# The memory projection moved behind the queries of tile zero, and all background work laid out in tables of slots

## The chip, the cores and the metric

The kernel runs on one core of one Trainium2 chip. The metric is the time of one execution on the device in microseconds (us). The core has five engines that run side by side: TensorE (PE, matmuls), VectorE (DVE), ScalarE (ACT), GpSimd (POOL) and SyncE (SP, which issues most of the DMA transfers, in order). The profile's granted clock is the share of TensorE's full speed that it was allowed.

## The reference

A decoder layer with one input projection, three groups of heads, a gate and an output projection, for 2048 rows of width 1024 in float32:

```
h = rms_norm(x, pre_norm_g);  proj = h @ w_in
a_u, a_v, sq, sk, sv, mq, z = split(proj)          # 512, 512, 256, 128, 128, 256, 1024 columns
y_a = gelu(a_u) * spatial_gating(gelu(a_v))        # A: layer norm per 128 channels, then causal 128x128 mixing over rows
y_b = sliding_window_attention(sq, sk, sv)         # B: 4 heads of 64, window 128, sinks, relative bias
mk, mv = split(rms_norm(mem, mem_norm_g) @ w_mem_kv)
y_c = memory_cross_attention(mq, mk, mv)           # C: 4 heads of 64 over 256 memory rows
y = concat(y_a, y_b, y_c) * silu(z)
out = x + rms_norm(y @ w_out, post_norm_g)
```

## The kernel before

The 2048 rows are worked in four tiles of 512 (L20). Every float32 operand of a large product is split into a high and a low part (ACT casts the high part, L107; DVE subtracts it, L108), and each product is three matmuls per 128 of depth: high by high, high by low, low by high. A unit is one such product of 128 output columns by a tile of 512 rows, 24 matmuls with a 128x512 result. The memory's units (gm, L494) have 256 columns of rows only.

Each tile runs its units in a fixed order: four units of v (L1076, with the rows as the stationary operand), sv, k, q0, q1, mq0, mq1 and the gates z4 to z7 (all in `group`, L388). In tile 0 the four memory units (`project_memory`, L487) stand between z5 and z6. Behind z7 of tiles 1 and 3 comes `set_a`: the u and z columns of group A, for two tiles together, with a Strassen-like scheme (28 products X, Y, Z at L819) on sums of blocks of h and of weights. The output projection (L1383) ends the kernel, with the same scheme, as a phase of its own from about 622 us.

The order on PE and SP is the order of the program. ACT, DVE and POOL are ordered by the language's scheduler, which lists each engine's instructions ahead of time from its own estimates, within the order that the data sets.

Background work hangs on slots. `slot()` is called after every 6 matmuls of a unit (about 1.4 us of PE). It sends the stores that have come due (`store_later` gives each a number of ticks), runs the jobs that are registered for this slot (`add_jobs`), and then the attention steps for it. Slot 0 of a tile is the start of its q1, and slots -28 to -1 are the tile's v, sv, k and q0. The jobs are: the row statistics of the next tile (`next_stats`: load a piece of x as xs, square and sum it on ACT at L311, reciprocal root on POOL, two small transfers), the raw rows of the next tile (`load_x`, xk and xj) and their scaling and splitting into h (`make_h`, L371), sums of h blocks (`h_sums`, hd and hr) and of weights (`weight_sums`, tu and tz), first sums of y (`first_sums`, ya at L767, ys2), operands of the output weights (`weight_operands`, wo, L697), and the operands of the last phase (`y_operand`). An attention unit has three steps: logits and softmax, transposes into pT, and the product with the values into OB or OC. B runs 4 units and C 8 per tile, and C of a tile runs on under v, sv and k of the next tile.

Weights come through a ring. `weight_unit` (L224) is called as a unit starts. It frees the place of the unit before, takes the raw weights of a later unit into that place, and issues the next raw load; there are three ring places and, in tile 0, a fourth (s4a), and three raw tiles. In tile 0 a raw block of 0.5 MB is loaded (L197), split, and its split form of 1 MB is stored to split_d (L243); tiles 1 to 3 load the split form at once (L205), which a place can only take when its former unit is done. All these transfers stand in SP's one queue with the jobs' transfers, in the order of the program; where SP waits for one transfer's data or place, all behind it wait.

In names, `hs` are the four resident buffers of split rows, `s4a` and `s4b` two spare ones. `wraw_0_8` is the raw weight of unit 8 in tile 0; units 0 to 3 are v, 4 sv, 5 k, 6 and 7 q, 8 and 9 mq, 14 to 17 z4 to z7, and 30 to 33 the memory's. `xs_1_4` is piece 4 of the rows of tile 1 for their statistics.

## Time and profile before

| | |
|---|---|
| runs shown | 787.1, 786.89, 782.41 us; median 786.89 |
| profiled execution | 783.41 us, span 781.7 us |
| mean granted clock | 0.984 |
| busy over the span | PE 746.3 us, DVE 576.8, ACT 481.4, POOL 93.4 |
| data moved by DMA | 220.19 MB, mean 282 GB/s |

The profile is one execution. Busy times are sums per engine; PE is busy for 95% of the span, so its idle time, and the time in which its clock was granted less, are the two quantities to follow. A row of the timeline shows when an instruction (or a run of like ones) began, how long it took, its engine, line and tiles, and in brackets how long the engine had been idle and what ended that. A row of waits shows who waited for what, with the total in us, the number of times and the longest.

### The profile page before, as it was taken

Reading aid. Unit: us, or ns where it says so; the run is one execution under the profiler, and the core shown is the slowest. Engines: PE = TensorE matmul, PEld = TensorE weight load, DVE = VectorE, ACT = ScalarE, POOL = GpSimd, SP = SyncE. Lnnn points to the kernel's source line nnn. Section 1 sums busy time; section 2 is a strip of 40 time slices with the busy share of each in tenths; the row PEclk is TensorE's granted clock in tenths of the full one; section 3 lists DMA queues with packets and bytes.
Section 4 is the critical chain, followed back from the end, with each engine's and each line's share of the span. In section 5 each row is a group of like instructions: output and inputs, shape, how many; then the busy total and the mean of one; then the engine's idle time right before and its main releaser. Section 6 shows DMA issues by size and latency. Waiting matters only on the chain.

```text
span 781.7 us, 10655 instructions
## 1 busy us (share of the span) xinstructions
PE 746.3 (95%) x3604; PEld 620.7 (79%) x3604; DVE 576.8 (74%) x1070; ACT 481.4 (62%) x1048; POOL 93.4 (12%) x115
## 2 busy tenths in 40 slices
PE   9999989889899999989998989999999999999996
PEld 7878968668778888867886768888887888888884
DVE  6665887588986779833797876898658818677587
ACT  7796856984479954236575795588853334434441
POOL 0110212110221000010043010141000000010011
PEclk9999989999999999999999999999999999999999
DMA  8999298996894587789979969986457889547824
GB/s 326 354 337 395 92 408 316 368 325 216 312 318 139 181 280 263 264 296 388 371 280 359 354 243 337 366 295 215 152 184 251 281 335 405 212 145 282 329 106 188
DMA packets 80646, 220.19 MB, mean 282 GB/s; under 512 B 7723, under 2 KB 16464, under 8 KB 72144
## 3 DMA queue, kind: packets, MB, share of 16 engines
q1 hardware_dynamic: 75456, 210.54, 74.6%
q10 hardware_dynamic: 5136, 8.98, 3.1%
q8 instruction: 28, 0.46, 0.2%
q14 instruction: 26, 0.21, 0.1%
HBM read 153.42 MB, written 66.07 MB: 281 GB/s over the span
## 4 chain that ended last, share of the span: by engine, by line
PE 53%; DMA 16%; DVE 14%; ACT 12%; issue 2%; SPq 2%; POOL 1%; DVEq 0%; ACTq 0%; POOLq 0%
PE X L1383 11%; PE X L819 11%; PE Y_S L1383 6%; PE Y L819 5%; DMA ring<-split_d 4%; PE Y L1383 3%; PE Z L819 3%; PE g_q L388 2%; PE v L1076 2%; PE g_mq L388 2%; DMA xp<-in_x 2%; DMA wraw_a<-in_wst 2%; PE sg L785 1%; DVE hs L108 1%; ACT G_v L1103 1%
## 5 line engine op out<-in xcount | busy, mean ns | idle before, releaser
L1076 PE MATMUL v<-ring,hs 128*128 128x512 f32 x336 | 86.6, 409 | 7.9 <-DMA ring<-split_d 3.6
L388 PE MATMUL g_z<-hs,ring 128*128 128x512 f32 x360 | 88.0, 394 | 3.6 <-DMA ring<-split_d 3.6
L1076 PEld LDWEIGHTS v<-ring,hs 128*128 128x128 f32 x336 | 64.3, 197 | 23.6 <-DMA ring<-split_d 4.0
L388 PEld LDWEIGHTS g_z<-hs,ring 128*128 128x128 f32 x360 | 65.9, 188 | 17.0 <-DMA ring<-split_d 4.2
L819 PE MATMUL X<-hs,ring 128*128 128x512 f32 x288 | 71.4, 395 | 0.0
L819 PEld LDWEIGHTS X<-hs,ring 128*128 128x128 f32 x288 | 52.3, 188 | 10.2 <-DVE hs L108 0.2
L388 PE MATMUL g_mq<-hs,ring 128*128 128x512 f32 x192 | 45.0, 390 | 0.0
L388 PE MATMUL g_q<-hs,ring 128*128 128x512 f32 x168 | 42.7, 405 | 1.5 <-DMA ring<-split_d 1.5
L108 DVE TENSOR_TENSOR ring<-wraw_a,ring 128x1024 fp32r<-128x1024 f32 x28 | 35.4, 1263 | 11.1 <-ACT ring L107 9.8
L388 PEld LDWEIGHTS g_mq<-hs,ring 128*128 128x128 f32 x192 | 35.8, 188 | 7.3
L594 POOL TENSOR_SCALAR_AFFINE_SELECT pT_b<-pT_b 128x512 fp32r<-128x512 f32 x30 | 25.9, 862 | 126.1 <-ACT pT_b L107 126.0
L1276 POOL TENSOR_TENSOR r<-a,mhalf 128x1 f32<-128x1 f32 x16 | 12.8, 802 | 231.5 <-DVE a L1274 226.8
L388 PEld LDWEIGHTS g_q<-hs,ring 128*128 128x128 f32 x168 | 31.6, 193 | 8.2 <-DMA ring<-split_d 1.9
L108 DVE TENSOR_TENSOR ring<-wraw,ring 128x1024 fp32r<-128x1024 f32 (+1 forms) x18 | 21.6, 1202 | 16.8 <-ACT ring L107 16.7
L1383 PE MATMUL Y_S<-hs,yop 128*128 128x512 f32 x144 | 33.1, 389 | 0.0
L107 ACT CAST ring<-wraw_a 128x1024 fp32r<-128x1024 f32 x28 | 29.3, 1047 | 5.0 <-DMA wraw_a<-in_wst 3.9
L581 ACT ACTIVATE Lc_b<-Lc_b,nm_b 128x129 f32<-128x129 f32 x64 | 25.0, 395 | 11.8 <-DVE nm_b L579 11.5
L1383 PEld LDWEIGHTS Y_S<-hs,yop 128*128 128x128 f32 x144 | 27.0, 188 | 5.6
L1383 PE MATMUL X<-hs,yop 128*128 128x512 f32 x120 | 30.4, 389 | 0.0
L1383 PE MATMUL X<-hs,ring 128*128 128x512 f32 x120 | 30.4, 389 | 0.0
L1244 ACT ACTIVATE junk<-oa 128x512 f32<-128x512 f32 x16 | 10.1, 633 | 32.8 <-DVE oa L1430 23.6
L1240 DVE TENSOR_TENSOR yop<-y,yop 128x1024 fp32r<-128x1024 f32 x10 | 12.2, 1221 | 24.0 <-ACT yop L1235 24.0
(277 smaller groups left out, 1823.5 us busy)
## 6 DMA issues: line engine op xcount, KB each, us to landing
ring<-split_d SPq DMA_DIRECT2D x38, 1024.0 KB, 8.0
split_d<-ring SPq DMA_DIRECT2D x11, 1024.0 KB, 10.0
wraw<-in_wst SPq DMA_DIRECT2D x21, 512.0 KB, 5.8
hs<-wo_B SPq DMA_DIRECT2D x8, 1024.0 KB, 9.8
y<-yd SPq DMA_DIRECT2D x8, 1024.0 KB, 6.0
xs<-in_x SPq DMA_DIRECT2D x24, 256.0 KB, 7.8
hd_S<-h SPq DMA_DIRECT2D x24, 256.0 KB, 4.6
hrS<-hd_S SPq DMA_DIRECT2D x24, 256.0 KB, 4.8
```

The costliest lines, as they stand in the source:

```text
L107: a = nc.scalar.copy(hi, src)
L108: b = (lo_engine or nc.vector).tensor_tensor(lo, src, f32(hi), ALU.subtract)
L388: nc.tensor.matmul(ps, w[:, wi, k * P : (k + 1) * P], h(t, hi, k), start=(n == 0), stop=(n == 3 * KC - 1))
L581: nc.scalar.activation(Lc[:, h, : P + 1], Lc[:, h, : P + 1], AF.Exp, bias=nm[:, h : h + 1], accum_out=den[:, h : h + 1])
L594: nc.gpsimd.affine_select(prev[:, s], f32(own[:, s]), [[0, 4], [-1, P]], ALU.is_gt, 0.0, base=0, channel_multiplier=1)
L785: nc.tensor.matmul(pg[:, i, :], vg[:, i, :], wsp[:, g, :], start=True, stop=True)
L819: nc.tensor.matmul(banks[g], w[:, wi, k * P : k * P + P], at_slot(places[op], hi, k), start=first and i == 0, stop=i == 11, skip_group_che ...
L1076: nc.tensor.matmul(vps[i], h(t, hi, 2 * j + kk)[:, i * P : (i + 1) * P], w[:, wi, kk * 512 : (kk + 1) * 512], start=(j == 0 and (hi, wi, k ...
L1240: nc.vector.tensor_tensor(w[:, 1], yraw[name, p][:, 2 * half : 2 * half + 2], f32(w[:, 0]), ALU.subtract)
L1244: nc.scalar.activation(junk, o[:, c], AF.Square, accum_out=ss[:, col : col + 1])
L1276: nc.gpsimd.tensor_tensor(r, a, mhalf2[:, 0:1], ALU.pow)
L1383: nc.tensor.matmul(banks[m], a(s, k)[:, m * P : (m + 1) * P], w(v, k), start=first and n == 0, stop=n == 11, skip_group_check=not first)
```

## The change

Three things are changed; each matmul, each transfer and each step of ACT and DVE stays what it is, but for ACT's loads of function tables, which follow from its order.

First, the memory projection (`memory_along`, `project_memory`) in tile 0 stands right behind q1, in slots 4 to 11, so that mq0, mq1 and z4 to z7 follow it. The order of the weights is changed with it. The splitting of the memory rows into mT (`next(prep)`), which stood ahead of mq0 and mq1, stands behind sv and behind k.

Second, all slots of background work are numbers in tables, where formulas set them before. `STATS`, `SQUARES` and `RSTD` replace a common list with an offset for each tile; `A_STARTS`, `A_TURN` and `A_END` give each attention unit its three steps; `H_SUMS`, `H_LOADS`, `H_OPS`, `H_SPARE`, `T_SLOTS`, `T_STEPS`, `Y_SUMS`, `Y_OPS`, `Y_WEIGHTS` and `WO_LOADS` those of the sums and operands. `LOADS`, `MAKES`, `MIX_SLOTS` and `WO_SLOTS` exist before and have other numbers.

Third, `STORE_AFTER` goes from 6 to 11, and `PUT_OFF` and `H_STORE` give each kind of store its own ticks.

```diff
-STORE_AFTER = 6
+STORE_AFTER = 11
-TURN_SLOT = 30
+TURN_SLOT = 19
...
-NEXT_STATS = (-8, 18, -23)
+STATS = ((-10, -6, 0, 1, 5, 8, 12, 15), (18, 21, 25, 28, 33, 35, 39, 42), (-23, -24, -16, -12, -9, -5, 0, 1))
...
-MAKES = ((32, 33, 35, 36, 38, 39, 41, 42), (66, 68, 70, 72, 76, 79, 85, 88), (20, 22, 24, 26, 29, 31, 33, 35))
+MAKES = ((33, 34, 36, 37, 39, 40, 42, 39),
+         (65, 67, 68, 71, 75, 78, 84, 87),
+         (17, 19, 21, 23, 26, 28, 30, 32))
...
         order += [(U_V + j, t) for j in range(4)] + [(U_SV, t), (U_K, t), (U_Q, t), (U_Q + 1, t)]
-        order += [(U_MQ, t), (U_MQ + 1, t), (U_Z + 4, t), (U_Z + 5, t)]
         if t == 0:
             order += [(U_MK, t), (U_MK + 1, t), (U_MV, t), (U_MV + 1, t)]
-        order += [(U_Z + 6, t), (U_Z + 7, t)]
+        order += [(U_MQ, t), (U_MQ + 1, t)] + [(U_Z + 4 + i, t) for i in range(4)]
...
         for n in range(12):
-            aw, dw, bw, cw, am, bm, cm = A_SLOTS[t]
-            a, b, c = (aw + dw * n, bw, cw) if n < 4 else (am + 3 * (n - 4), bm, cm)
+            a, b, c = A_STARTS[t][n], A_TURN[t][n], A_END[t][n]
...
         SB.append(split_heads(slotted(U_Q + 1, f"q{t}_1", False), f"q{t}_1", "S1"))
         slot()
+        if t == 0:
+            memory_along()
+            project_memory(late["mT"], slot)
         for i in range(2):
-            if t == 0:
-                late["mT"] = next(prep)
             SC.append(split_heads(slotted(U_MQ + i, f"mq{t}_{i}", False), f"mq{t}_{i}", f"S{2 + i}"))
...
-        gate_bc(0)
-        gate_bc(1)
-        if t == 0:
-            memory_along()
-            project_memory(late["mT"], slot)
-        gate_bc(2)
-        gate_bc(3)
+        for i in range(4):
+            gate_bc(i)
```

What the tables do is read from the order of the instructions. The first place is ACT during the v units of tile 1. `G_v1_0` to `G_v1_3` are the gelus of v's four row blocks, `L_c` the softmax of attention C of tile 0, and an `ACT_TABLE_LOAD` loads the function table that the next step needs. Before:

```order
L660 ACT_TABLE_LOAD
L660 ACTIVATE G_v1_0_1510<-v_1_0_1231 128x512
L632 ACT_TABLE_LOAD
L632 ACTIVATE L_c0_1_1_1443,den_c0_1_1_1445<-l_c0_1_1_1438,nm_c0_1_1_1444,rsr_x0_273 128x256 x2
L660 ACT_TABLE_LOAD
L660 ACTIVATE G_v1_1_1533<-v_1_1_1232 128x512
L107 CAST pT_c0_0_0_1429<-tp_c0_0_1_1467 128x2x256
L549 ACTIVATE L_c0_1_1_1443<-L_c0_1_1_1443,den_c0_1_1_1445 128x256 x2
L1103 ACTIVATE G_v1_0_1510<-G_v1_0_1510,nb_1_0_1526,rsr_v1_0_1524 128x128 x4
L632 ACT_TABLE_LOAD
L632 ACTIVATE L_c0_2_0_1490,den_c0_2_0_1492<-l_c0_2_0_1485,nm_c0_2_0_1491,rsr_x0_273 128x256 x2
```

And now:

```order
L696 ACT_TABLE_LOAD
L696 ACTIVATE G_v1_0_1518<-v_1_0_1228 128x512
L696 ACTIVATE G_v1_1_1541<-v_1_1_1229 128x512
L145 CAST pT_c0_0_0_1461<-tp_c0_0_0_1456 128x2x256
L585 ACTIVATE L_c0_1_1_1432<-L_c0_1_1_1432,den_c0_1_1_1434 128x256 x2
L145 CAST pT_c0_0_0_1461<-tp_c0_0_1_1464 128x2x256
L696 ACTIVATE G_v1_2_1564<-v_1_2_1230 128x512
L696 ACTIVATE G_v1_3_1587<-v_1_3_1231 128x512
L668 ACT_TABLE_LOAD
L668 ACTIVATE L_c0_2_0_1488,den_c0_2_0_1490<-l_c0_2_0_1483,nm_c0_2_0_1489,rsr_x0_273 128x256 x2
L689 COPY oh_c0_0_1_1514<-o_c0_0_1_1509 64x512
```

All four gelus stand between two table loads; before, four loads are in the rows shown, and two more surround the gelus of `G_v1_2` and `G_v1_3` further down.

The second place is SP's queue at the start of tile 2's sv. `ring0` from `split_d` (first of the two) is the weight of sv, `ya` are parts of y read back for the first sums. Before:

```order
L306 DMA xs_3_0_3321<-in_x 128x512
L767 DMA ya_11_3329<-yd_107 128x2x512
L767 DMA ya_21_3330<-yd_107 128x2x512
L767 DMA ya_22_3331<-yd_107 128x2x512
L205 DMA ring0_84<-split_d_88 128x2048
L306 DMA xs_3_1_3348<-in_x 128x512
L205 DMA ring1_85<-split_d_88 128x2048
```

And now:

```order
L343 DMA xs_3_1_3315<-in_x 128x512
L343 DMA xs_3_0_3323<-in_x 128x512
L242 DMA ring0_84<-split_d_88 128x2048
L802 DMA ya_11_3357<-yd_107 128x2x512
L802 DMA ya_21_3358<-yd_107 128x2x512
L802 DMA ya_22_3359<-yd_107 128x2x512
L242 DMA ring1_85<-split_d_88 128x2048
```

The weight's load has moved ahead of the three `ya` loads, and `xs_3_1` ahead of it.

The third place is SP's queue in tile 0, under q and the units that follow it. Before:

```order
L243 DMA split_d_88<-ring2_86 128x2048
L306 DMA xs_1_2_576<-in_x 128x512
L197 DMA wraw_0_15_593<-in_wst 128x1024
L243 DMA split_d_88<-s4a_87 128x2048
L306 DMA xs_1_3_616<-in_x 128x512
L197 DMA wraw_0_30_639<-in_wst 128x1024
L243 DMA split_d_88<-ring0_84 128x2048
L306 DMA xs_1_4_662<-in_x 128x512
L197 DMA wraw_0_31_685<-in_wst 128x1024
L243 DMA split_d_88<-ring1_85 128x2048
```

And now:

```order
L280 DMA split_d_88<-ring2_86 128x2048
L234 DMA wraw_0_33_607<-in_wst 128x1024
L280 DMA split_d_88<-s4a_87 128x2048
L343 DMA xs_1_2_617<-in_x 128x512
L343 DMA xs_1_3_626<-in_x 128x512
L234 DMA wraw_0_8_652<-in_wst 128x1024
L343 DMA xs_1_4_680<-in_x 128x512
L234 DMA wraw_0_9_692<-in_wst 128x1024
L234 DMA wraw_0_14_730<-in_wst 128x1024
L343 DMA xs_1_5_745<-in_x 128x512
```

The memory's weights (30 to 33) have come ahead of those of mq (8, 9) and of the gates (14 and on), with no store of a split block behind them, and the reloads of `xs` stand at other places among them.

More of the change, by code (lines that the diff above doesn't have):

```diff
@@ L323, in from_dram @@
             nc.sync.dma_start(late["bcs", t], rstd_d[t : t + 1].broadcast_to([P, TS]))
-        for n, s in enumerate((0, 3, 7, 10, 14, 17, 21, 24)):
-            yield s, lambda n=n: load(n)
-            yield s + 6, lambda n=n: square(n)
-        yield 31, rstd
-        yield 33, to_dram
-        yield 36, from_dram
+        for n in range(8):
+            yield STATS[t - 1][n], lambda n=n: load(n)
+            yield SQUARES[t - 1][n], lambda n=n: square(n)
+        for s, job in zip(RSTD[t - 1], (rstd, to_dram, from_dram)):
+            yield s, job
     def along(rstd, t):
@@ L703, in operand @@
                     split(w[:, 0, c], w[:, 1, c], r[raw][:, c])
-            store_later(wo_d[op][j], f32(w), 4)
+            store_later(wo_d[op][j], f32(w), PUT_OFF[0])
         def difference(new, a, b, at):
@@ L911, in combine @@
             if name:
-                store_later(hsum_d[p][name][k], r[into, k], 2)
+                store_later(hsum_d[p][name][k], r[into, k], H_STORE[p])
         def operand(name, slot, k):
@@ L1127 @@
         slot()
+        if t == 0:
+            late["mT"] = next(prep)
         ps = group(weight_unit(U_K, t), t, f"k{t}", ps_t)
@@ L1136 @@
         slot()
+        if t == 0:
+            late["mT"] = next(prep)
         def values():
```

122 lines of the change are left out of this document (72 added, 50 removed), and 19 rows, old and new, of tables (A_END, A_STARTS, A_TURN, H_SUMS).

## The prediction

> **What bounds the kernel now.** I read the page's busy shares first, then the busy time by stage, then the list of what TensorE (PE) waited for, and last the timeline at each wait.
>
> ```profile
> PE 746.3 (95%) x3604; PEld 620.7 (79%) x3604; DVE 576.8 (74%) x1070; ACT 481.4 (62%) x1048; POOL 93.4 (12%) x115
> core 0: us, PE busy (x) PEld busy (x) DVE busy (x) ACT busy (x) POOL busy (x), PEclk, DMA share, GB/s
> 0.00:100.00 100.00, 98.47 (x500) 83.34 (x501) 67.38 (x150) 78.50 (x157) 12.57 (x23) 1.00 0.82 302
> 100.00:180.00 80.00, 70.16 (x328) 55.72 (x328) 61.77 (x142) 60.61 (x130) 12.73 (x13) 0.94 0.91 339
> 180.00:340.00 160.00, 156.42 (x787) 131.74 (x786) 123.79 (x201) 94.34 (x217) 14.99 (x19) 1.00 0.74 250
> 340.00:420.00 80.00, 72.42 (x335) 59.79 (x334) 54.11 (x128) 48.12 (x122) 17.41 (x20) 0.96 0.94 347
> 420.00:600.00 180.00, 174.64 (x878) 145.71 (x877) 141.27 (x270) 129.66 (x296) 22.91 (x24) 0.99 0.78 275
> 622.00:782.00 160.00, 152.22 (x672) 125.72 (x670) 108.51 (x153) 62.53 (x117) 12.83 (x16) 0.99 0.67 252
> ```
>
> PE is the bound: it is idle 781.7 - 746.3 = 35.4 us. Of that 7.8 lies in the last stage, the output projection, which the change doesn't touch, and 1.5 ahead of the first matmul. About 26 us are left, spread over four stages (9.8, 3.6, 7.6, 5.4). After some of the waits the granted clock is below 1, so that the matmuls behind them are slow as well. The changed kernel issues the same matmuls, so these waits and their slow matmuls are all that it can win, and new waits are all that it can lose.
>
> ```profile
> PE g_z L388 <- DMA ring<-split_d: 3.6, 2, 2.4
> PE v L1076 <- DMA ring<-split_d: 3.6, 1, 3.6
> PE v L1076 <- ACT hs L107: 2.6, 2, 1.7
> PE svt L1141 <- DVE OC L655: 2.6, 1, 2.6
> PE g_sv L388 <- DMA ring<-split_d: 2.5, 1, 2.5
> PE l_c L622 <- ACT L_c L632: 2.5, 2, 1.9
> PE v L1076 <- DVE hs L108: 1.6, 3, 0.8
> PE Y L819 <- DVE s4b L108: 1.6, 1, 1.6
> PE g_q L388 <- DMA ring<-split_d: 1.5, 1, 1.5
> PE g_k L388 <- ACT L_c L632: 1.4, 1, 1.4
> PE o_c L650 <- ACT pT_c L107: 1.2, 1, 1.2
> ```
>
> These are total, count and longest. There are two kinds: weights that land late (ring<-split_d), where SyncE's (SP's) single queue issued them late, and background steps on ACT and DVE (h, exp, OC) that end late. Both hang on the order in which slots issue work, which is what the change lays out anew.
>
> ```profile
> 111.74 4.11 PE L1076 MATMUL v<-ring,hs 128*128 128x512 f32 x9 [0.41 <-DVE hs L108]
> 346.41 7.41 PE L388 MATMUL g_sv<-hs,ring 128*128 128x512 f32 x24 [2.52 <-DMA ring<-split_d]
> 353.66 5.60 PE L388 MATMUL g_k<-hs,ring 128*128 128x512 f32 x24
> 415.88 2.86 PE L1076 MATMUL v<-ring,hs 128*128 128x512 f32 x6 [3.57 <-DMA ring<-split_d]
> ```
>
> The same 24 matmuls take 5.60 us undisturbed and 7.41 behind a wait of 2.52: the slow clock costs 1.8 on top. By the same rate nine should take 2.1 and took 4.11 (2.0 lost), six should take 1.4 and took 2.86 (1.5 lost).
>
> For this there is a rule. The Trainium skill, "TensorE: Matmul & The Clock Gate", in "Why this matters for your kernels", says that the clock drops where TensorE idles for over about 3 us. By that rule waits of 0.4 to 2.5 us would cost no clock, and removing them would not bring the slow matmuls back. The trace differs: 7.41 against 5.60 behind 2.52 us. The rows decide, and the rule's outcome is a rival below.
>
> **The change part by part.** The places go in order of time; each ends with a value and its bounds.
>
> (1) Tile 1's first product, 106 to 116. The waits for h are 3.5 (2.6 + 1.6, less 0.8 of tile 3), and the clock 2.0.
>
> ```profile
> 106.25 1.03 ACT L107 CAST ring<-wraw 128x1024 fp32r<-128x1024 f32 x1
> L108 DVE TENSOR_TENSOR hs<-xk,hs 128x512 fp32r<-128x512 f32 x16 | 12.0, 756 | 0.4 <-ACT hs L107 0.3
> ```
>
> A 1.03 us weight cast stands right ahead of the first h cast on ACT; in the new order it stands two copies and a softmax step earlier, and the memory values' steps (L523/L524), which lie among them before, are long done. On DVE the two low halves of h (0.76 each) still stand behind z7's scaling, which needs the end of z7, so about 1.3 us of wait stays. Gain 3.5, bounds 1.5 and 5.5.
>
> (2) Attention C of tile 0, under v, sv and k of tile 1, 140 to 172. That is 9.8 - 3.5 = 6.3 us of idle (l_c and svt the largest).
>
> ```profile
> 140.00:150.00 10.00, 7.75 (x37) 5.71 (x36) 4.71 (x18) 9.35 (x21) 2.02 (x2) 1.00 1.05 399
> 150.00:160.00 10.00, 9.09 (x45) 6.83 (x43) 8.05 (x32) 8.57 (x17) 1.58 (x2) 1.00 0.96 358
> 160.00:170.00 10.00, 6.81 (x28) 5.22 (x28) 9.72 (x22) 9.91 (x26) 0.82 (x1) 0.84 0.84 278
> L660 ACT ACT_TABLE_LOAD x8 | 10.3, 1283 | 0.1
> L632 ACT ACT_TABLE_LOAD x5 | 6.4, 1283 | 0.1
> ```
>
> ACT is busy 27.8 of 30 us here. Six of its steps are table loads of 1283 ns, since gelu and exp alternate; in the new order the four gelus of tile 1 stand together and two loads are left, so ACT has 4 x 1.28 = 5.1 us less to do ahead of the steps that PE waits for. The clock of 0.84 over 6.81 busy us costs 1.1. DVE is full from 160 on and still carries h sums, so I don't take all of 7.4: gain 5, bounds 2.5 and 7.4.
>
> The Trainium skill, "ScalarE: Activation LUTs", in "What ACT_TABLE_LOAD costs", adds a drain of about 1.38 us to each load of 1.28. By that, as an estimate, four loads would be worth 10.6 us of ACT, all of this place's 7.4 would go, and the sum below would be 2.4 lower. The trace agrees on the load (1283), and shows 0.2 us of idle before all thirteen loads of these two lines, so no drain.
>
> (3) z5 and z7 of tile 1, 199 to 218: 3.6 us for late weights.
>
> ```profile
> 193.73 0.32 SPq L205 DMA_DIRECT2D ring<-split_d  x1
> ring<-split_d SPq DMA_DIRECT2D x38, 1024.0 KB, 8.0
> ```
>
> z5's load left SP at 193.73 and landed 8.0 later, at 201.7, just as PE started. Ahead of it stood four h loads and the loads tu_3 and tz_3; now two of the h loads and those two stand behind it, but h sums of k=2 still stand ahead of z7's load. Gain 2.5, bounds 0 and 3.6.
>
> (4) sv and q1 of tile 2, 343 to 367: 2.5 + 1.5 of wait, 1.8 of clock.
>
> ```profile
> 336.47 1.99 SPq L767 DMA_DIRECT2D ya<-yd  x3
> 338.55 0.41 SPq L205 DMA_DIRECT2D ring<-split_d  x1
> ```
>
> sv's load stood behind three ya loads, which SP held until 336.47 for their data, and left at 338.55, 5.3 us before PE needed it. In the new order it stands ahead of them. What it needs then is only its place, which the second product of v gave up two units of about 5.5 before 343.9, at 333; so the wait of 2.5 and its clock go. q1's load now stands behind xs_3_3 and xs_3_4, so its 1.5 may stay. Gain 4, bounds 1.5 and 5.8.
>
> (5) v of tile 3 at 412: 3.6 of wait, 1.5 of clock.
>
> ```profile
> SPq L360 <- DVE hs L108: 25.9, 5, 9.4
> 407.87 1.07 SPq L205 DMA_DIRECT2D ring<-split_d  x1
> ```
>
> The load left at 407.87, behind xk_3_2, which waited for DVE to make h of k=0. That step is three slots earlier now and ahead of two weight subtractions: about 4 us. Gain 4, bounds 2 and 5.1.
>
> (6) Attention C under tile 3's v, sv and k: 0.8 + 1.2 + 1.4. The makes of h are earlier, and the last two gelus stand behind an exp and the svs copy, which releases pT_c and L_c sooner. Gain 3, bounds 0 and 3.4.
>
> (7) Y at 593: 1.6 for s4b. Its DVE step now follows the addition into u directly, without the two steps that stood between. Gain 1.5, bounds 0 and 1.6.
>
> (8) The memory projection, now right behind q1 in tile 0.
>
> ```profile
> L494 PE MATMUL gm<-hs,ring 128*128 128x256 f32 x72 | 9.3, 285 | 0.0
> split_d<-s4a SPq DMA_DIRECT2D x3, 1024.0 KB, 10.1
> 54.28 11.04 PE L388 MATMUL g_mq<-hs,ring 128*128 128x512 f32 x48
> SPq L306 <- ACT xs L311: 43.7, 12, 7.9
> ```
>
> Its matmuls are half as wide: a unit lasts about 3 us, where one of mq lasts 11.04 / 2 = 5.5. Four units therefore use up four weight blocks in 12 us, not 22, and the fourth (gm_3) gets the place of q1's weights, whose store takes 10.1 us to land. That store comes into SP's queue as q1 starts, one unit ahead of 54.28, at about 48.5, behind one raw load; landed by 59 to 60, it lets ACT cast at 60 to 61. gm_3 starts three units of 3 behind 54.28, at 63.3, and a cast and a subtraction (about a microsecond each, as at place 1) lie between: 0 to 1.5 us late. I take 1.5, the late end, since a late load slows the clock too. Nothing below zero is possible, since this stage has no wait at present (98.5 busy of 100, with 1.5 before the first matmul). The work on mT stands where it stood on ACT and DVE, hidden under sv and k; I cost it at nothing, as I do the stores that leave 11 ticks behind their step rather than 6: they only hold their tiles longer, and PE doesn't read those. Without that cover it is one of the waits of (9).
>
> (9) New waits that I haven't named: nearly every background step moves, so one load will come late somewhere; the rows above give 2.4 to 3.6 for one. Take one, 3, bounds 0 and 6 (two).
>
> Sum against the profiled execution's own 783.4 (span 781.7 and 1.7 around it): 3.5 + 5 + 2.5 + 4 + 4 + 3 + 1.5 = 23.5 of gain, 1.5 + 3 = 4.5 of loss: 783.4 - 19.0 = 764.4. The profiled execution lies 3.5 below the median of the runs shown (786.89) and 1.0 above their lowest. I add half of the 3.5: **766**. One per cent, about what a measurement of this kernel can tell from no change, puts the bounds at 779.0 and 794.8.
>
> **The rivals.** *Nearly all goes.* Every gain at its upper bound, 32.4, and no new wait: 783.4 - 32.4 = 751.0, and with the same 1.7 about 753. For it speaks that most waits are below 3 us; against it that DVE is busy 9.72 of 10 at 160. Chance 0.07.
>
> *The waits go, the slow clock stays.* The clock terms are 2.0 + 1.1 + 1.8 + 1.5 = 6.4; at the share taken above, about 5 of them would not come back: 771. It decides if slow stretches come without waits ahead of them. Against it stands that every slow stretch found follows a wait. This is the outcome by the clock rule of the Trainium skill named above. Chance 0.07.
>
> *Other waits in their place.* DVE, not ACT, sets the end at (1), (2), (5) and (6): 9.72 of 10 busy there. Then their 15.5 shrinks to 4, (3), (4) and (7) give 8, and a denser start and later stores bring 9 of new waits: 783.4 - 12 + 9 = 780. It decides where DVE's steps in that order end no earlier than before. Chance 0.16.
>
> *SP blocks the weights.* SP issues in order, and a reload of xs waits for ACT's square of the tile's previous content: 43.7 us over 12 times, up to 7.9. In the new order xs_1_4 stands ahead of the raw loads of mq1 and z4, behind the square of xs_1_2, which stands behind gm_3's late cast on ACT. If that hold reaches 7.9, with about 2 us to spare, mq1 starts 5.9 late, plus 1.8 of clock: 7.7. The same pair (xs ahead of a weight load) is set in tiles 1 and 2: three times make 23, and with only (3) and (4) gained (6.5) that gives 783.4 + 23 - 6.5 = 800. It decides from 2 us of hold, and pays above 795 once the three holds together pass 18. For it speaks the 43.7; against it that those waits cost PE nothing in tile 0 at present. Chance 0.10.
>
> **How the numbers follow.** The forecast itself has 0.60, with a range of its own of 756 to 777 (gains and losses don't reach their ends together). Faster by over 1%: 0.60 + 0.07 + 0.07 = 0.74; within 1%: 0.16; slower: 0.10. The range 755 to 784 leaves out the case where nearly all goes and the slower one, 0.17, and reaches through most of the case in which other waits take over.
>
> **What would show it.** In the changed kernel's profile: twelve table loads' rows in place of sixteen, two of them at 140 to 160; sv of tile 2 and v of tile 3 with no wait for ring<-split_d over 1 us, and 24 matmuls of sv in about 5.6; z5 of tile 1 likewise; under 2 us of wait ahead of tile 1's first h; and in 54 to 75 at most 1.5 of idle. PE idle in all about 17, not 35. I would be wrong if PE waits for gm or mq weights in 60 to 80 for more than 3 us, if svt still waits for OC at 165, or if the idle time adds up to 30 with other names in it.

## The result, and the profile after

The changed kernel takes 761.3 us (median of 4 runs, 760.16 to 765.02) beside 784.65 for the kernel before (782.0 to 787.1): a ratio of 0.9711, with a 95% interval of 0.9657 to 0.9766. The profiled execution took 760.56 us with a span of 758.8, at a mean granted clock of 0.993.

First the page's busy shares of the changed kernel:

```profile
PE 738.4 (97%) x3604; PEld 616.6 (81%) x3604; DVE 572.3 (75%) x1070; ACT 477.0 (63%) x1044; POOL 88.6 (12%) x115
```

Then its busy time in the same stretches of time as before (the columns as in the prediction). The changed kernel runs ahead of the kernel before, so a stretch now holds more of the work (352 matmuls in the first, where 328 were):

```profile
100.00:180.00 80.00, 73.06 (x352) 59.25 (x351) 64.39 (x147) 56.48 (x126) 11.97 (x14) 0.96 0.91 338
180.00:340.00 160.00, 159.24 (x797) 133.45 (x797) 123.47 (x221) 96.38 (x221) 15.64 (x20) 1.00 0.79 272
340.00:420.00 80.00, 76.84 (x388) 64.80 (x387) 59.61 (x123) 54.78 (x141) 18.81 (x23) 1.00 0.96 348
420.00:600.00 180.00, 179.41 (x910) 150.94 (x909) 149.18 (x282) 128.12 (x283) 16.63 (x20) 1.00 0.79 284
```

The same 3604 matmuls are busy for 738.4 us, not 746.3: 7.9 us are matmuls that no longer run at a slow clock. PE is idle 758.8 - 738.4 = 20.4 us, not 35.4: 15.0 less (the prediction's sign was about 17). Together that is the 22.9 us between the two spans. Almost nothing is left to win in 180 to 340 and 420 to 600 (0.8 and 0.6 us of idle). The stage from 100 to 180 still holds 6.9.

The list of what PE waited for in the changed kernel (total, times, longest):

```profile
PE v L1109 <- ACT hs L145: 4.2, 2, 4.0
PE g_q L424 <- DMA ring<-split_d: 1.6, 1, 1.6
PE v L1109 <- DMA ring<-split_d: 1.6, 1, 1.6
PE svt L1178 <- DVE OC L691: 1.2, 1, 1.2
PE o_c L686 <- DVE pT_c L146: 1.0, 1, 1.0
PE X L854 <- DVE ring L146: 0.8, 1, 0.8
PE Y L854 <- DVE s4b L146: 0.3, 1, 0.3
```

Both waits of the gates for weights, the wait of sv and that of l_c are gone. The largest that is left is tile 1's first product, and it is longer than before. By the prediction's places, with waits and slow matmuls taken together (us):

| place | before | after | gain | forecast |
|---|---|---|---|---|
| 1 tile 1's first product | 3.5 + 2.0 | 4.5 + 1.8 | -0.8 | 3.5 |
| 2 attention C of tile 0, 140 to 172 | 6.3 + 1.1 | 2.4 | 5.0 | 5 |
| 3 z5 and z7 of tile 1 | 3.6 | 0 | 3.6 | 2.5 |
| 4 sv and q1 of tile 2 | 4.0 + 1.8 | 1.6 | 4.2 | 4 |
| 5 v of tile 3 | 3.6 + 1.5 | 1.6 | 3.5 | 4 |
| 6 attention C under tile 3 | 3.4 | 0.2 | 3.2 | 3 |
| 7 Y behind s4b | 1.6 + 1.4 | 0.3 | 2.7 | 1.5 |
| 8 memory projection | 0 | 0 | 0 | -1.5 |
| 9 new waits | 0 | 0.8 | -0.8 | -3 |
| sum | | | 20.6 | 19.0 |

The 2.3 us that remain of the 22.9 are 0.4 of idle and 1.9 of slow matmuls that I haven't put down to a place.

Place 1, on PE's timeline of the changed kernel:

```profile
110.86 0.79 PE L1109 MATMUL v<-ring,hs 128*128 128x512 f32 x1 [3.99 <-ACT hs L145]
111.90 1.34 PE L1109 MATMUL v<-ring,hs 128*128 128x512 f32 x2 [0.25 <-ACT hs L145]
113.48 3.88 PE L1109 MATMUL v<-ring,hs 128*128 128x512 f32 x9 [0.24 <-DVE hs L146]
```

Three waits make 4.5 us, and the nine matmuls behind them take 3.88 instead of 2.1. What they wait for is seen in ACT's rows of the same timeline:

```profile
100.28 1.05 ACT L145 CAST s4a<-wraw 128x1024 fp32r<-128x1024 f32 x1 [2.28 <-DMA split_d<-s4a]
103.56 0.63 ACT L702 ACTIVATE Z_z<-sc_z 128x512 f32<-128x512 f32 x1 [2.23 <-DVE sc_z L433]
105.72 1.04 ACT L145 CAST ring<-wraw 128x1024 fp32r<-128x1024 f32 x1
110.19 0.62 ACT L145 CAST hs<-xk 128x512 fp32r<-128x512 f32 x1 [1.04 <-DVE xk L407]
```

The weight cast does stand well ahead of the first h cast, at 105.72. But the cast of h waits for its scaling on DVE. In the kernel before, that cast stood right behind the weight cast, at 107.18, and the scaling of its two pieces had begun only at 105.83:

```profile
105.83 1.78 DVE L371 SCALAR_TENSOR_TENSOR xk<-xk,colt,bcs 128x512 f32<-128x512 f32 x2
```

The first piece is done at 106.57, so even there the weight cast held the first cast of h by 0.6 us at most, and the scaling set the rest. In the changed kernel ACT and DVE wait for each other in turn: the cast into s4a waits until the store out of s4a has landed; DVE's subtraction for it, and the scaling of z6 behind that, come late; with them the softmax on ACT, the weight cast and its subtraction; and h's scaling at 109.41 is at the end. The start of this chain is in SP's rows:

```profile
82.84 9.04 SPq L396 DMA_DIRECT2D xk<-in_xT  x2
93.39 0.42 SPq L280 DMA_DIRECT2D split_d<-s4a  x1
```

SP stood for 9.0 us at the load of xk, whose place is that of the last piece of xs; it came free with ACT's square of that piece at 90.81, itself behind a weight cast. The raw weights and the store out of s4a stood behind it.

### The profile page after: what moved, and what is told of

Its sections match the earlier page's. It is cut to its first block, busy times and chain, and to the rows that moved or that the text cites. A ratio compares the mean times of both kernels' runs of the same rounds, so it can differ in the third digit from the quotient of the medians.

```text
span 758.8 us, 10655 instructions
## 1 busy us (share of the span) xinstructions
PE 738.4 (97%) x3604; PEld 616.6 (81%) x3604; DVE 572.3 (75%) x1070; ACT 477.0 (63%) x1044; POOL 88.6 (12%) x115
## 4 chain that ended last, share of the span: by engine, by line
PE 73%; DVE 14%; ACT 6%; DMA 5%; issue 2%; SPq 0%; DVEq 0%; POOL 0%; ACTq 0%; POOLq 0%
PE X L854 12%; PE X L1416 11%; PE v L1109 10%; PE Y_S L1416 6%; PE Y L854 5%; PE g_q L424 4%; PE g_z L424 3%; PE g_mq L424 3%; PE Y L1416 3%; DMA ring<-split_d 3%; PE Z L854 3%; PE sg L820 2%; PE l_c L658 2%; DVE hs L146 2%; PE gm L530 2%
## 5 line engine op out<-in xcount | busy, mean ns | idle before, releaser
L1109 PE MATMUL v<-ring,hs 128*128 128x512 f32 x336 | 84.9, 406 | 6.0 <-ACT hs L145 4.2
L424 PE MATMUL g_q<-hs,ring 128*128 128x512 f32 x168 | 41.1, 395 | 1.6 <-DMA ring<-split_d 1.6
L630 POOL TENSOR_SCALAR_AFFINE_SELECT pT_b<-pT_b 128x512 fp32r<-128x512 f32 x30 | 22.5, 751 | 124.6 <-ACT pT_b L145 124.6
L146 DVE TENSOR_TENSOR ring<-wraw,ring 128x1024 fp32r<-128x1024 f32 (+1 forms) x18 | 20.9, 1164 | 20.6 <-ACT ring L145 20.6
L585 ACT ACTIVATE L_c<-L_c,den_c 128x256 f32<-128x256 f32 x64 | 29.2, 509 | 3.0 <-DVE den_c L583 3.0
L146 DVE TENSOR_TENSOR pT_c<-tp_c,pT_c 128x512 fp32r<-128x512 f32 x32 | 22.0, 686 | 12.2 <-ACT pT_c L145 11.9
```

Source lines behind the costliest of these rows:

```text
L146: b = (lo_engine or nc.vector).tensor_tensor(lo, src, f32(hi), ALU.subtract)
L424: nc.tensor.matmul(ps, w[:, wi, k * P : (k + 1) * P], h(t, hi, k), start=(n == 0), stop=(n == 3 * KC - 1))
L585: last = nc.scalar.mul(p[:, e, :], p[:, e, :], den[:, e : e + 1])
L630: nc.gpsimd.affine_select(prev[:, s], f32(own[:, s]), [[0, 4], [-1, P]], ALU.is_gt, 0.0, base=0, channel_multiplier=1)
L1109: nc.tensor.matmul(vps[i], h(t, hi, 2 * j + kk)[:, i * P : (i + 1) * P], w[:, wi, kk * 512 : (kk + 1) * 512], start=(j == 0 and (hi, wi, k ...
```

## The experiments

Each kernel is the changed one with one part undone or altered, but for two, which are the kernel before with one part of the change alone. Times are medians; a ratio is to the kernel before, run beside it, with its 95% interval.

**The square that SP waits for, earlier.** The last square of tile 1's rows moves three slots ahead.

```diff
-SQUARES = ((-2, 1, 4, 7, 12, 15, 17, 22),
+SQUARES = ((-2, 1, 4, 7, 12, 15, 17, 19),
```

> The changed kernel, with one number of a table changed: the square of the last piece of tile 1's rows (xs_1_7) at slot 19 of tile 0, not 22. Theory A: in the changed kernel SP stood for 9.0 us at the load of xk_1_1, whose place that square frees, so that the store of the spare weight block left late, its next cast on ACT waited 2.3 us for the store, and the casts of tile 1's first h came late: 4.5 us of wait and about 2 of slow clock at 106 to 118. Then SP stands there for less than 5 us, the waits at tile 1's first product fall to 2 us or less, and the time falls by 3 to 5 us, to 756 to 758. Rival B: the wait is set by DVE's order (h's steps behind z7's scaling). Then SP stands shorter, but more than 3 us of wait remain and the time is within 1.5 us of the changed kernel's.

Measured: 760.13 us (759.96 to 760.31), ratio 0.9686 (0.9661 to 0.9712). On the timeline, SP's row for the load of xk, and PE's first product:

```profile
82.41 2.14 SPq L396 DMA_DIRECT2D xk<-in_xT  x2
```

```profile
109.35 0.80 PE L1109 MATMUL v<-ring,hs 128*128 128x512 f32 x1 [2.94 <-ACT hs L145]
```

The hold shrinks from 9.0 us to 2.1, and s4a's cast no longer waits for a store, but the first wait falls by only 1.05. More than 3 us of wait remain (2.94 and two of about 0.25), and the time moves by 1.2 us, within the spread of the changed kernel's runs: that is Rival B, and the 2 us or less of Theory A didn't come. In the profile a new wait for l_c (2.3) stands where the one for svt (1.2) was.

What SP's hold costs is more than this one pair of profiles shows. Four kernels below (the attention steps, the first sums of y, the makes of the third group and the stores) have the changed kernel's order on ACT, DVE and SP up to this place, and their first product waits 5.17, 4.07, 5.60 and 5.21 us. The cast into s4a waits there for its store 3.49, 2.36, 3.91 and 3.54 us, as in the third of them:

```profile
101.35 1.05 ACT L145 CAST s4a<-wraw 128x1024 fp32r<-128x1024 f32 x1 [3.91 <-DMA split_d<-s4a]
```

The first wait is 1.7 us longer than the cast's in all five kernels, the changed one with 3.99 and 2.28 among them. So while the cast stands for its store, the first product follows it one for one, and in one and the same order the landing of that store moves this place by 1.6 us. Without the hold 2.94 us are left here and 2.69 in the last experiment: it costs 1.05 to 2.7 us, and DVE's own work sets the rest. DVE is busy for 11.85 of the 13 us from 100 to 113 here, and for 9.80 in the changed kernel, where it waits for the late cast.

**xk one slot later**, as before the change.

```diff
-LOADS = ((23, 23, 29, 29, 30, 35), ...
+LOADS = ((24, 24, 29, 29, 30, 35), ...
```

> The changed kernel, with the loads of xk_1_0 and xk_1_1 one slot later (24, not 23), so that they stand behind the raw weight wraw_1_1 and the store of the spare block in SP's queue. ACT's order gets 14 table loads instead of 12, the two more at tile 1's gelus. Theory A (the blocked SP queue makes tile 1's first product late): its waits fall from 4.5 to 2 us or less. Theory C (table loads cost PE time under attention C): the waits at 140 to 172, 2.4 us in the changed kernel, rise by 1.5 to 2.6 us. Both: the time changes by -3 to 0 us. Rivals: without A no fall at 106 to 118; without C no rise at 140 to 172.

Measured: 766.22 us (766.16 to 766.42), ratio 0.9765 (0.9739 to 0.979): 4.9 above the changed kernel, where 0 to 3 less was expected. The cast into s4a waits for nothing here (it starts at 97.21), and yet the first product waits 3.59, so without SP's hold most of that wait stays in this order too. This order has fourteen table loads, two more than the changed kernel, and under k:

```profile
154.03 2.90 PE L424 MATMUL g_k<-hs,ring 128*128 128x512 f32 x6 [2.26 <-issue]
```

Place 2 waits 3.9 us instead of 2.4. That is 1.5 for two loads of 1.28, the direction that Theory C asks for, but no proof of it: the profile names nothing that PE waited for in the 2.26 (`issue`), and the kernel with the early square waits 3.5 us at place 2 with twelve loads. A slow six (2.90, where the changed kernel's under k take 1.64) comes on top.

**The attention steps by the old formulas.**

```diff
-A_STARTS = ((14, 19, 24, 29, 38, 41, 44, ...), (7, 12, 17, 22, 29, 31, 34, ...), ...
-A_TURN = ((8, 8, 8, 8, 12, 8, 8, ...), (6, 8, 8, 8, 8, 8, 7, ...), ...
-A_END = ((13, 13, 14, 13, 11, 10, 13, ...), (11, 14, 13, 14, 7, 10, 10, ...), ...
+A_STARTS = ((14, 19, 24, 29, 38, 41, 44, ...), (7, 12, 17, 22, 28, 31, 34, ...), ...
+A_TURN = ((8, 8, 8, 8, 8, 8, 8, ...), (8, 8, 8, 8, 7, 7, 7, ...), ...
+A_END = ((13, 13, 13, 13, 11, 11, 11, ...), (13, 13, 13, 13, 10, 10, 10, ...), ...
```

> The changed kernel with the attention steps in the slots of the kernel before (the tables A_STARTS, A_TURN and A_END filled by the old formulas); ACT's order has 16 table loads again. Theory C (table loads and the C units' slots gave 5 us at 140 to 172 and 3 at 430 to 460): the waits at the two places rise by 4 to 7 us together, and the time by 5 to 9 us, to 766 to 770. Rival: the two places were relieved by what was moved away from ACT and DVE there (casts, h sums); then the waits rise by under 2 us and the time by under 2 us.

Measured: 778.68 us (777.4 to 778.84), ratio 0.9919 (0.9892 to 0.9947): 17 us above the changed kernel, more than either theory gave. The longest of PE's waits:

```profile
PE v L1100 <- ACT hs L136: 5.4, 2, 5.2
PE l_c L649 <- ACT L_c L659: 4.9, 2, 2.5
PE g_k L415 <- ACT svs L1150: 4.2, 1, 4.2
PE Y L845 <- DVE s4b L137: 2.2, 1, 2.2
```

The sixteen table loads are back, and so are the waits at the places 2, 6 and 7, at 4.9, 4.2 and 2.2. The first product's 5.2 lies ahead of any change of order, so its 1.2 above the changed kernel aren't the attention's. The attention tables are a necessary part of the gain.

**The first sums of y at their old slots.**

```diff
-Y_SUMS = ((-18, -11, -9), (-14, -7, -5))
+Y_SUMS = ((-22, -15, -13), (-12, -5, -3))
```

> The changed kernel with the first sums of y in their old slots (loads at -22 and -12, not -18 and -14); in SP's queue the three ya loads stand ahead of the weight of tile 2's sv again. Theory D (sv waited because its load stood behind the ya loads): sv waits 2 to 3 us for its weight at about 327 to 331 and its matmuls run slow, so the time rises by 3 to 5 us, to 764 to 766. Rival: the load was late for its place or for full DMA queues; then sv waits under 1 us and the time is within 1 us.

Measured: 765.5 us (764.02 to 767.64), ratio 0.9764 (0.9727 to 0.9801). On the timeline, SP's rows, and sv on PE:

```profile
328.39 2.02 SPq L802 DMA_DIRECT2D ya<-yd  x3
330.45 1.61 SPq L242 DMA_DIRECT2D ring<-split_d  x2
```

```profile
338.03 5.73 PE L424 MATMUL g_sv<-hs,ring 128*128 128x512 f32 x24 [0.90 <-DMA ring<-split_d]
```

With the three ya loads ahead of it again, sv's weight leaves at 330.45, not 326.00, and comes late again, but by 0.9, not 2.5, and its 24 matmuls aren't slowed. So the queue order does what place 4 said, with less than the 2 to 3 us of Theory D. The time rises by 4.2, as that theory gave, but by other ways: v of tile 3 waits 2.5 instead of 1.6, with a slow six behind it, and a gate's weights are 1.1 late.

**The attention tables alone**, in the kernel before.

```diff
-            aw, dw, bw, cw, am, bm, cm = A_SLOTS[t]
-            a, b, c = (aw + dw * n, bw, cw) if n < 4 else (am + 3 * (n - 4), bm, cm)
+            a, b, c = A_STARTS[t][n], A_TURN[t][n], A_END[t][n]
```

> The kernel before, with nothing changed but the attention steps' slots (the new A_STARTS, A_TURN and A_END). ACT's order has 14 table loads, four instead of six around tile 1's gelus. The run without the new attention slots lost 17 us of the 24 that the change gains. Theory F (the attention tables carry the gain by themselves): this run is 12 to 18 us faster than the kernel before, near 769. Theory G (the tables only fit together: every background step shares ACT's and DVE's order, and none of the tables is worth its place without the others): it is under 7 us faster, and waits return under other names.

Measured: 788.17 us (10 runs, 786.33 to 795.9), ratio 1.0056 (1.0028 to 1.0083): what loses 17 us when taken out wins nothing when put in. The longest of PE's waits:

```profile
PE v L1086 <- DMA ring<-split_d: 5.1, 1, 5.1
PE g_z L399 <- DMA ring<-split_d: 3.9, 2, 3.0
PE g_sv L399 <- DMA ring<-split_d: 3.9, 1, 3.9
PE l_c L633 <- ACT L_c L643: 3.9, 2, 3.2
PE tp_c L650 <- ACT L_c L643: 3.1, 1, 3.1
```

The late weights are all still there, longer than before (5.1, 3.9 and 3.9 instead of 3.6, 3.6 and 2.5), and attention C waits no less (l_c and tp_c alone 7.0). ACT, with the old makes and sums around these steps, gets fourteen table loads, not twelve. So the theory that each table brings its own share falls.

**The memory projection alone**, in the kernel before: the order of units, `TURN_SLOT` and the place of `project_memory` are those of the change, and all other slots are as before.

> The kernel before, with the memory projection moved behind q1 of tile 0 (its weights, the mT steps and the turn of the values with it) and all other slots as before. Theory E (the move by itself is worth little: tile 0 has no wait to lose, and memory's steps only leave ACT and DVE earlier): within 3 us of the kernel before, at most 1.5 us of wait in 54 to 75, and tile 1's first product waits up to 2 us less than its 3.5. Rival H (weights become late in tile 0): 3 us or more of wait in 54 to 80, and slower by 3 us or more.

Measured: 789.98 us (787.7 to 790.26), ratio 1.0057 (1.0039 to 1.0076). Busy time in the stretch of the memory projection:

```profile
50.00:106.00 56.00, 56.00 (x324) 49.28 (x322) 40.05 (x69) 44.93 (x108) 6.97 (x9) 1.00 0.72 270
```

And the largest wait that before did not have:

```profile
PE o_b L603 <- POOL pT_b L595: 2.5, 4, 1.3
```

PE is busy 56.00 of 56.00 there: no memory weight comes late, and Rival H falls. But the 5.2 us above the kernel before are more than the 3 of Theory E. In the profile, 4.3 us longer than that of before, the window attention of tiles 1 and 3 (o_b and tp_b) waits 3.7 us, where it waited 0.3, and q1 of tile 2 waits 0.9 longer, with 1.4 more of slow matmuls; other waits got shorter.

**The memory projection back** between z5 and z6, with all other tables of the change.

```diff
-TURN_SLOT = 19
+TURN_SLOT = 30
...
+        gate_bc(0)
+        gate_bc(1)
+        if t == 0:
+            memory_along()
+            project_memory(late["mT"], slot)
+        gate_bc(2)
+        gate_bc(3)
```

> The changed kernel, with the memory projection back between z5 and z6 and all the new tables kept (only the turn of the last values at its old slot 30). Theory E: within 3 us of the changed kernel, 758 to 764. Theory G (the tables fit this place of the memory): slower by 4 us or more, with the waits at 100 to 120.

Measured: 763.73 us (762.0 to 764.92), ratio 0.973 (0.9702 to 0.9758), 2.4 above the changed kernel in the median, with intervals that overlap, as Theory E gave. The splitting of the memory rows stays behind sv and k here. So the move of the projection by itself can't be told from nothing.

**The sums of h and of weights (first group, tu and tz) at their old slots.**

```diff
-T_SLOTS = (32, -13, -6, 9)
+T_SLOTS = (28, -20, -10, 5)
...
-T_STEPS = ((6, 8, 10, 12, 12), (8, 10, 12, 14, 14), (6, 8, 10, 12, 12), (2, 2, 6, 8, 8))
+T_STEPS = ((6, 8, 10, 12, 12),) * 4
```

(and the first group of `H_SUMS`, whose later entries move by up to three slots)

> The changed kernel with the first h sums and the weight sums in their old slots (H_SUMS for tiles 0 and 1, T_SLOTS, T_STEPS). In SP's queue the weight of tile 1's z5 stands behind all four h loads and tu_3 and tz_3 again. Theory I (z5 and z7 of tile 1 waited because their loads stood behind those): z units wait 2 to 3.6 us again at 195 to 215, and the time rises by 2 to 5 us. Rival: less than 1 us of wait there and the time within 1.5 us.

Measured: 774.0 us (770.41 to 775.82), ratio 0.9857 (0.9821 to 0.9893). The two largest of PE's waits:

```profile
PE v L1106 <- ACT hs L142: 9.0, 1, 9.0
PE g_z L421 <- DMA ring<-split_d: 6.1, 3, 3.9
```

DVE's row of h's scaling, and below it the busy time of that stretch:

```profile
113.49 1.77 DVE L404 SCALAR_TENSOR_TENSOR xk<-xk,colt,bcs 128x512 f32<-128x512 f32 x2
```

```profile
112.00:120.00 8.00, 3.01 (x5) 1.69 (x6) 8.00 (x12) 4.05 (x6) 1.99 (x3) 0.50 0.92 369
```

The gates' weights come late again (6.1), as place 3 said. The time rises by 12.7, not by the 2 to 5 us of Theory I, because place 1 suffers too: three subtractions of weight blocks into s4b (0.68, 0.68 and 1.10 us) stand ahead of h's scaling, which begins 4.1 us later (113.49 instead of 109.41), 1.3 of it because the cast into s4a begins that much later already. The first product waits 9.0, DVE is full (8.00 of 8.00), and PE runs at half its clock. So the new slots of the weight sums keep place 1 from being worse.

**The whole of h earlier in tile 1**: square, reciprocal root and the first two makes.

```diff
-SQUARES = ((-2, 1, 4, 7, 12, 15, 17, 22),
+SQUARES = ((-2, 1, 4, 7, 12, 15, 17, 19),
-RSTD = ((23, 24, 30), ...
+RSTD = ((20, 21, 26), ...
-MAKES = ((33, 34, 36, 37, 39, 40, 42, 39),
+MAKES = ((28, 29, 36, 37, 39, 40, 42, 39),
```

> The changed kernel with three numbers or pairs of tile 0's tables changed: the last square at slot 19 (22), the row statistics' reciprocal root and its two transfers at 20, 21 and 26 (23, 24 and 30), and the first two pieces of tile 1's h made at 28 and 29 (33 and 34). On DVE h's scaling then stands ahead of the softmax of the last window unit and its low halves ahead of z7's scaling; on ACT its casts stand ahead of that unit's softmax. 12 table loads as in the changed kernel. Theory B2 (with SP's block gone, 3.4 us of wait at tile 1's first product were left because h stood behind that softmax and z7): the waits there fall below 1 us and no slow clock follows, 5 to 6 us less than the changed kernel at 106 to 118; the time falls to 754 to 757, if the later order stays as good. Rival: the scaled rows' factor (bcs) lands too late for it, DVE waits for that, and a wait of 2 us or more stays at 106 to 118.

Measured: 762.09 us (760.09 to 764.31), ratio 0.971 (0.9678 to 0.9741). On the timeline, rows of PE, DVE and ACT:

```profile
106.83 2.88 PE L1109 MATMUL v<-ring,hs 128*128 128x512 f32 x12
113.29 1.36 PE L623 MATMUL tp_b<-ident,Lc_b 128*128 128x128 f32 x4 [3.57 <-ACT Lc_b L585]
106.69 0.68 DVE L433 TENSOR_TENSOR sc_z<-g_z,bcs 128x512 f32<-128x512 f32 x1
107.40 0.63 ACT L702 ACTIVATE Z_z<-sc_z 128x512 f32<-128x512 f32 x1 [3.52 <-DVE sc_z L433]
```

And the busy time of that stretch:

```profile
100.00:113.00 13.00, 9.72 (x49) 7.94 (x47) 12.07 (x19) 6.24 (x16) 5.64 (x6) 0.99 1.02 413
```

The first product waits for nothing now. Twelve matmuls on, the transposes of the last window unit wait 3.57 us for their softmax, because z6's scaling on DVE comes at 106.69, behind the steps of h, ACT waits 3.52 for that, and the softmax is behind it on ACT. The six of v behind them take 2.91 us. So Theory B2 fails: the wait has only changed its name. What binds here is how much DVE has to do: it is busy for 12.07 of the 13 us, and was for 11.81 in the kernel before, while ACT is busy for 6.24. (DVE did wait 1.43 us for bcs, as the rival said, but PE didn't wait there.)

**The makes of the third group at their old slots**, with SP's order unchanged.

```diff
-         (17, 19, 21, 23, 26, 28, 30, 32))
+         (20, 22, 24, 26, 29, 31, 33, 35))
```

> The changed kernel with tile 3's h made at the old slots (20, 22, ... 35, not 17, 19, ... 32). The order in SP's queue is the same in both; only DVE and ACT differ. Theory J (v of tile 3 waited 3.6 us because SP stood for DVE's making of xk_3_0): v's wait for its weight at about 403 rises from 1.6 to 3 to 4 us, its first matmuls run slow, and the time rises by 2 to 4 us. Rival: the weight's place or the wo stores ahead of it set that wait; then it stays below 2 us and the time within 1 us.

Measured: 764.15 us (762.83 to 765.74), ratio 0.9738 (0.9707 to 0.9769). The load for v of tile 3 on SP, and v on PE, here:

```profile
396.50 0.93 SPq L242 DMA_DIRECT2D ring<-split_d  x1
405.12 2.93 PE L1109 MATMUL v<-ring,hs 128*128 128x512 f32 x6 [3.33 <-DMA ring<-split_d]
```

And in the changed kernel:

```profile
394.09 0.92 SPq L242 DMA_DIRECT2D ring<-split_d  x1
402.37 1.65 PE L1109 MATMUL v<-ring,hs 128*128 128x512 f32 x6 [1.55 <-DMA ring<-split_d]
```

The load leaves 2.4 us later, the wait goes back to 3.3, and a slow six follows, as place 5 and Theory J said: SP's queue is the same, and only the make of h, which gives xk's place free ahead of this load, has other slots. The medians are 2.9 apart, with runs that overlap; of the 4.9 us by which the two profiles differ, 1.6 is the first product of tile 1, where the order is the same. Place 6 has no wait in this profile, so the earlier makes aren't what relieved it.

**Stores at their old ticks.**

```diff
-STORE_AFTER = 11
+STORE_AFTER = 6
-H_STORE = (1, 2)
+H_STORE = (2, 2)
-PUT_OFF = (4, 1, 4, 6, 6, 4)
+PUT_OFF = (4, 2, 4, 6, 6, 4)
```

> The changed kernel with the stores' delays of before (STORE_AFTER 6, not 11; weight sums and h sums after 2 ticks). No step of ACT, DVE or PE is another; on SP the stores of z, of the sums and of hd stand at other places among the loads. Theory K (the stores' delays are worth nothing by themselves): within 2 us of the changed kernel. Theory G (each table fits the others): SP waits for sums that aren't ready and weights behind them come late, so 3 us or more slower, with waits for ring at 180 to 230.

Measured: 769.21 us (767.67 to 770.53), ratio 0.9796 (0.9752 to 0.9839), 8 us above the changed kernel. The order of ACT and DVE changes too from tile 1 on, against what was expected, so this is no measure of the stores alone. One of its waits:

```profile
PE mvt L555 <- ACT mvs L548: 1.8, 1, 1.8
```

It lies at 68 us, in the memory projection, ahead of any change of order; the changed kernel waits 0 there, and the kernel with xk later 0.8. So in one and the same order this place costs 0 to 1.8 us, from one execution to the next. With the first product's 5.2 instead of 4.0, which lies ahead of the change too, 3.0 of the 9.8 us between the two profiles come from places where the order is the same. No weight is late at 180 to 230, as Theory G had it, and Theory K's 2 us are passed, so neither is shown.

**The early square, and a load of xs out of q1's way.**

```diff
-STATS = (..., (-23, -24, -16, -12, -9, -5, 0, 1))
+STATS = (..., (-23, -24, -16, -12, -6, -5, 0, 1))
-SQUARES = ((-2, 1, 4, 7, 12, 15, 17, 22), ..., (-20, -17, -13, -10, -5, -3, 1, 4))
+SQUARES = ((-2, 1, 4, 7, 12, 15, 17, 19), ..., (-20, -17, -13, -10, -3, -2, 1, 4))
```

> The kernel with the early square of xs_1_7 (slot 19), and besides the load of xs_3_4 three slots later (-6, not -9; the squares of xs_3_4 and xs_3_5 at -3 and -2). In SP's queue the weight of tile 2's q1 then stands ahead of xs_3_4; ACT's order changes by one square. Theory L (q1's load left at 342.6 because SP stood for 5.5 us at the two xs loads): the load leaves about 4 to 5 us earlier, q1's wait of 1.3 us goes, and the time falls by 1 to 1.5 us against the kernel with the early square alone, to about 759. Rival: the load waits for its place or the wait moves to a later unit; then the time is within 0.5 us of 760.1.

Measured: 760.01 us (759.28 to 760.6), ratio 0.968 (0.9647 to 0.9713). The wait of q1 of tile 2 falls from 1.27 (with the early square alone) to 0.44, and v of tile 3 gets a new one of 0.47: the time is the same as with the early square alone, as the rival said. It has the lowest median, 1.3 us under the changed kernel, and their intervals overlap.

## Why the prediction was right, and where it wasn't

The forecast of 766 was 4.7 us high, and 761.3 lies in its range. The mechanism was right: the waits went, and the slow clock went with them (7.9 us less busy time for the same matmuls), so the rival in which the slow clock stays fell. That the sum by places came within 1.6 us is in part luck: place 1 falls 4.3 short of its forecast, and the losses of 8 and 9 that came out smaller give 3.7 back.

**Place 1 is the step that failed.** The prediction took the order of casts on ACT for the cause: a weight cast ahead of the first h cast. That cast did move ahead, and the wait grew from 3.5 to 4.5; its sign, under 2 us there, failed. In the kernel before, the weight cast had held h by 0.6 us at most. The runs put two things in its place: SP's hold of 9.0 us at xk, by way of the store out of s4a (1.05 to 2.7 us of the wait), and DVE's work between 100 and 113, which sends the wait to the window attention when h is made first. Here the rival "other waits in their place" held, with DVE in the end setting the time.

**Places 2 to 6 were right in size, and in part in their causes.** Place 2 gained 5.0, what four table loads would give (5.1). But no run takes the loads out alone, only three of the six loads lie in the 140 to 170 that the prediction looked at (the others begin at 135.06, 136.97 and 139.49), ACT is as busy from 140 to 172 as before (29.8 of 32 us), and kernels with twelve loads wait from 2.0 to 3.5 us there. So the loads as the cause stay argued. The attention slots as a whole are shown to be needed: at the old ones place 2 waits 6.1. And svt still waits for OC, 1.2 us instead of 2.6, which the prediction had named as a sign of being wrong. Of the twelve loads one lies at 140 to 160 (143.34) and one just ahead (138.19), where two were forecast. The two groups that had thirteen loads have nine:

```profile
L696 ACT ACT_TABLE_LOAD x6 | 7.7, 1283 | 0.1
L668 ACT ACT_TABLE_LOAD x3 | 3.8, 1283 | 0.0
```

The Trainium skill's drain of 1.38 us at each load ("ScalarE: Activation LUTs", "What ACT_TABLE_LOAD costs") would, by the prediction's estimate, have taken all 7.4 at place 2; it gained 5.0, and the idle before these nine loads is 0.1 in all, so the trace shows no drain. At place 3 the two waits went, and the old sums bring them back. At place 4 the wait of sv went and q1's stayed (1.6), as said; at place 5 1.6 stayed where I had taken 1.1, so the sign of no wait over 1 us failed there. Its clock term was taken too large: a row of six undisturbed lasts 1.5 to 1.6 us, not 1.4, so the slow six of 2.86 lost about 1.3. At place 6 the size was right, but the attention slots gave it (4.2 and 0.4 us come back with the old ones), not the makes.

**Place 7 was sized too small**, 1.5 where 2.7 came: I had not counted the matmuls at a lower clock behind it, in the kernel before

```profile
594.01 2.76 PE L819 MATMUL Z<-hs,ring 128*128 128x512 f32 x6
```

where six undisturbed take 1.54. With the old attention slots the wait is back, at 2.2, so it too hangs on more than the step that the prediction named.

**Place 8** was costed at its late end of 1.5 and cost nothing in the profiled execution; two others, with the same order up to there, wait 0.8 and 1.8 in it. Its bounds of 0 and 1.5 were about right by luck: the prediction priced a late weight of gm_3, which came in time in all three, and the waits are those of mvt for ACT's copy mvs. That the stores are free was wrong as far as it was tested: with the old ticks the kernel loses 8 us, though with another order of ACT and DVE mixed into it.

**Place 9** was sized at 3 and is 0.8. The rival in which SP blocks the weights named the right queue, and its holds came: SP waited for ACT's squares 26.6 us at xs, up to 8.8 at once, and 14.0 at xk. The hold at xk costs its share of place 1, and one of 5.6 us at two xs loads, 1.4 of it for a square, makes q1 of tile 2 late (the 1.6 of place 4; with the second of these loads behind q1's it is 0.4). The raw weights of mq1 and z4 held up no matmul, so the 7.7 us for each tile didn't come.

What the prediction lacked altogether is how the parts hang together. By the medians, undoing one part at a time costs 17.4 (attention), 12.7 (sums), 7.9 (stores), 4.2 (first sums), 2.9 (makes) and 2.4 (memory): 47.5 us together, twice the gain of 23.4. Runs of the last three overlap those of the changed kernel (760.16 to 765.02); without them it is still 38.0. Attention or memory alone on the kernel before loses 3.4 and 5.2. The prediction's sum by places came out, but no place belongs to one table. Left open is why the stores' ticks cost 8, and what part of it is the new order of ACT and DVE.

## What to carry to other kernels

Where background work hangs on slots and its engines are listed by a scheduler, price a new layout by the places where the main engine waits, not by the edits, and test a layout as a whole: its parts alone can lose. For a late step follow the chain over all engines to its first wait (here a store's landing, and SP held by a place not yet free); the instruction that stands right ahead of it in its own list is often not what it waits for. Where making it earlier only moves the wait to its neighbour, look whether an engine is busy through the whole stretch (here DVE, for 12.07 of 13 us). If so, less work for it there is the next thing to try; no run here tried it.

## What the runs showed of the hardware that I had not expected

Waits of much the same length slow the matmuls behind them at one place and not at another. Undisturbed, a row of 24 takes 5.60 us, and one of 12 takes 2.90 (under k in the changed kernel). In the kernel with the memory projection alone:

```profile
370.88 7.18 PE L387 MATMUL g_q<-hs,ring 128*128 128x512 f32 x24 [2.39 <-DMA ring<-split_d]
351.41 5.73 PE L387 MATMUL g_sv<-hs,ring 128*128 128x512 f32 x24 [2.15 <-DMA ring<-split_d]
201.74 3.02 PE L387 MATMUL g_z<-hs,ring 128*128 128x512 f32 x12 [3.27 <-DMA ring<-split_d]
```

A wait of 2.39 costs 1.6 us of clock, one of 2.15 next to nothing, and one of 3.27 only 0.1. In the kernel before, the 1.63 of place 7 cost 1.2 on the six matmuls shown there. So from about 1.6 to 3.3 us these rows don't decide it by the length of the wait. The Trainium skill, "TensorE: Matmul & The Clock Gate", says in "What's actually happening" that the clock follows activity in a window of about 3.4 us that runs freely. That would let a wait's place in the window decide, which would agree with rows of like length and unlike cost. But by that section's table the clock falls after a whole window of idle, longer than any of these waits, and the rule of about 3 us in "Why this matters for your kernels" doesn't fit the 1.63 and the 2.39 either. No run here shows the window itself.
